# Norm factors applied behind the output projection, memory probabilities turned by VectorE and by way of memory, and a new hand-written order

## The chip, the cores and the metric

The program runs on one core of a Trainium2 chip. A core has a matrix engine (PE, with its weight loads shown as PEld), VectorE (DVE), ScalarE (ACT), GpSimd (POOL) and SyncE (SP, which here only issues DMAs), each with its own in-order instruction queue. The metric is the device time of one execution in microseconds (us); lower is better.

## What is computed

One block of a hybrid model for a sequence of 512 tokens with width 1024: an RMS norm, one wide input projection, four mixers of width 512 next to each other, one output projection, and a last RMS norm.

```python
h = _rmsnorm(x, norm_g[l])
p_fox, p_ssm, p_nsa, p_mem = _split(h @ w_in[l], [FOX_COLS, SSM_COLS, NSA_COLS, MEM_COLS])
mem_kv = _rmsnorm(mem, mem_norm_g[l]) @ w_mem_kv[l]
o = jnp.concatenate([_fox_mixer(...), _ssd_mixer(...), _nsa_mixer(...), _mem_mixer(p_mem, mem_kv)], axis=-1)
x = x + o @ w_out[l]
return _rmsnorm(x, final_norm_g)
```

Two parts matter for the change. The second mixer (mixer 1, the state space mixer) ends in an RMS norm over two groups of 256 columns with a learned gain; the fourth (mixer 3, memory attention, 4 heads of 128) is a plain softmax over 256 memory tokens:

```python
yg = (y * jax.nn.silu(z)).reshape(B, S, SSM_GROUPS, GROUP_W // SSM_GROUPS)
return _rmsnorm(yg, norm_g.reshape(SSM_GROUPS, -1)).reshape(B, S, GROUP_W)
...
s = jnp.einsum('bshd,bmhd->bhsm', q, k).astype(jnp.float32)
pr = jax.nn.softmax(s, axis=-1).astype(v.dtype)
o = jnp.einsum('bhsm,bmhd->bshd', pr, v).reshape(B, S, GROUP_W)
return o * jax.nn.silu(gate)
```

## The kernel before, in words

**Products.** A product in full precision is made of three matmuls (`three`): each operand is split into a rounded high part and the rest (names with h and l: `hh`/`hl`, `wh`/`wl`, `oh`/`ol`). A weight block of 128x1024 is loaded as `raw` (512 KB, by SP), its high part `wh` is made by ACT, and the rest `wl` by a subtraction on POOL or DVE; three `raw`, three `wh` and three `wl` tiles are in turn. `pj` are the PSUM tiles of the input projection, `po` those of the output projection.

**Mixers.** Each mixer is a pipe of stages over its steps (class `Pipe`). The second mixer, `ssm`, has four steps c (128 tokens each). Its stage s3 makes the gated `yc`, s4 the two mean squares `pn` and from them the factors `rsr` (a power on POOL), and s5 spreads these along the free axis by 2 matmuls into PSUM (`prs`, `bcast_rows`) and multiplies four 128x128 pieces by gain and factor (`of<-yc,x,prs` on DVE). `of` is then split into `oh`, `ol`.

**Turning probabilities.** The matmul with the values needs the probabilities with the keys on partitions. In the first and third mixers (probabilities `pF`, `pN`) this is done in two halves: `flip` transposes 32x32 blocks on DVE (STREAM_TRANSPOSE into `fl`), `flip_out` writes each `fl` by 4 DMAs of 64 KB to a scratch tile `farN` in memory, in block order, and `flip_in` reads it back by one DMA of 256 KB as `pt`. In memory attention (`mem`, eight steps, head j and half b2, the probabilities `pM`) the constant MF = 0 lets stage s2 transpose by PE instead: four 128x128 transposes into PSUM (`pT<-cst,pM`), then the split into `pth` (ACT) and `ptl` (DVE). The stages s2o, s2i and s2p, which would go by way of memory for heads j < MF, do nothing.

**Output projection.** `out_proj(mixer, c)` runs over two pairs of token tiles t and over two weight blocks i; a PSUM tile `po` sums all four blocks f of 128 rows, and DVE adds it to the running sum `acc` (`acc<-acc,po`). The last mixer's part (`out_last`) also ends with the final norm.

**Order.** Nothing decides at run time. ORDER says in which order weight blocks are loaded and used; PLAN is a string of steps (a letter for a pipe and the number of its stage; `W` splits a weight block, `L` loads one, `.9` runs nine matmul steps of the foreground); PICKS says for each operation with a choice which engine takes it (V DVE, A ACT, P POOL). All engines' queues follow from the order in which the program text is run through.

Of the kernel before, what the change touches and what calls it, by code (L numbers as in the profile page):

```python
# [44 lines left out]
MF = 0  # L45
# [23 lines left out]
    "f2.5L0.1f3.1f0f2f0f0f2.3W0W0f2.4f3f1.2f1.4f2f2f4.5f3.1f3W0f0f4f0L0.6f4.2f5.1f1L0.3f3.1W0L0.4W0f4f1f0"
    "f2f0f1.6L0L0.5f3f3.6W0W0f0.2f1f1f2.1f2.2f4f4.1W0f3f3s0.1f4f1f4f0f0f0f1f1f1f4f2f2.2f3.5L0L0.4f5f2f2.1"  # L70
    "f2f3f2.4W0W0.6f4L0L0f0L0f3c0.1W0.3f5.1f3f5f5f5f3.5W0.9.1f4f4f5.4f4f4O0f1f5f5L0.1s0s0.3L0f2s1s1.5W0.2"
    "f5W0.2f5f5f3f3s2f5c1f4f5s3f4f5B0f5O0c2O0W0.1O0s1.9.3s0L0W0.3s2s2c3s3L0s3.2L0L0.5s4s1.9.2W0W0.3s2L0s5"
    "W0s3B0B0B0.2L0.3s4L0s4s4.1B0.1W0.9.6W0W0s5s5s5n0n0.7L0.2L0n1.3W0W0.2L0L0L0n0n1n0.1n1.3n2n2n2.8n1W0n3"
    "n0.1n1W0.5n2W0L0n3n4n4n2.4n0n0n3n5n5n3L0.8n1n1W0L0n4n0.2O1O1.2n2.3n3.3n2.2W0.1n3n0.1n0n0n1n1.3O1.3L0"
    ".1L0.3n2W0W0n5.2n1n1n0n0n4n4n4.4L0.1n2W0O1.7n1n1n3n4n2n2n3n3n2n0L0.2n3n3n0n5.5W0n5n3n2.4L0.1n5n3n0n4"
    "n4.1n5n5.4n0n1n4n4n0L0n1n1W0n2n0n2n4.3n1.1n2.3n5L0.4W0.3n5.4n2W0n5n5.3n1n1n3n0n0n0.8L0L0.1n3W0n2n1n1"
    ".4n3n3n3.3n1n4n4n4n4.1W0n5n2W0n5n5n5n0n0n0n0.3n1.1n4.1n2n2.1n2.2L0n3.3W0.9n3.1n1n3.2B0n4n4.2n0L0L0n2"
    ".3L0n4.1n4n1W0n1n2n5n5n3.1W0.2n5.3n0n0n3n1n3.8n2.1n0.3n0W0L0L0n2.5n2n1n5n1n4n4n4n3n1W0n3n3n0n2.2n2n1"
    "n4n4.1n3.3n4W0.9n2.3L0m0m0L0m0.2W0L0.3W0.2n1m1n5m1n5n5n5n4m1n2.2n5n5O2n5n3n3m2.1n2W0.4m2.1m3.1m2.1m3"
    "m3m4n4m0m0m0m0n5m4m4n3n5.1n3.1m5m5O2m1m1n4.1n4m2L0n4n5n5m2L0m1m3m6n5L0m2m5O2O2m3m3m0.2m4.1W0.4m4.5W0"  # L80
    "m4.3m5m5m5m1m1m2W0m6m6m2m3m3.1L0.1L0.3m4m4L0.2m6.4W0.4m6m6.1m5m5.1W0.2m6m6.2W0.9.9.9.9.1"
# [5 lines left out]
    "Rk": "AVVAAVVV",
    "Rl": "VAAAAAVA",
    "ce": "PPVVVV",
    "ct": "AVAAVAVVAAVAVVVA",  # L90
    "kh0": "AVV",
    "kh1": "AVV",
    "ll": "PVPVPPVV",
    "m": "PVVPVPVV",
    "ml": "PVPV",
    "ol": "VVPVPPVPVPPVPPV",
    "pF": "VVVVVVVAVAVVVVAVAAVVVVVAAVVVAVVV",
    "pM": "VAAVVVAAVAVVVAVA",
    "pN": "AVVVAAVVAVAAAAVAVAVAVAAAVVVVVAAVAAVAVVAAAVVVAVAVAAAVAVVAVVAAVVVV",
    "sq": "VPVPVPPV",  # L100
    "wl": "PVPPPPPPPPPPVVVPVPVPPVVVPPPVPPVVPVVPVPPVPVPPVVPVPPVPPPPVVPPPPPVPVPVPPPVV",
    "xde": "VVV",
    "xp": "VVPVVVVV",
    "yc": "PVVVVVVVVVVPVVVP",
# [2047 lines left out]
```

## Time and profile before

| | us |
|---|---|
| median of 3 runs (lowest to highest) | 511.45 (511.14 to 514.05) |
| the profiled execution's own time | 511.3 |
| its span in the trace | 509.5 |
| PE busy | 496.4 |
| DVE busy | 368.9 |
| ACT busy | 297.3 |
| POOL busy | 164.4 |

The span goes from the first to the last instruction of the trace; 1.8 us of the execution's time lie outside it. Busy times are sums over the instructions of an engine, so an engine can be busy for 97% of the span while its instructions overlap. In rows, `out<-in` names the tile written and those read, without their numbers; all lines are L360 since one helper records every operation, and so the tile names tell what an instruction is.

### The profile page before, as it was taken

How to read it: one execution, taken by the hardware profiler on the slowest of the kernel's cores; microseconds unless marked ns; L12 is line 12 of the kernel's file. 1: busy time of each engine (PE TensorE's matmuls, PEld its weight loads, DVE VectorE, ACT ScalarE, POOL GpSimd, SP SyncE). 2: the span in 40 equal slices, each digit the busy share in tenths (PEclk: the TensorE clock that was granted, in tenths of full speed). 3: DMA queues.
4: the chain of work that ended last, by engine and by line, in shares of the span. 5: the costliest groups of instructions: out<-in, count | busy, mean ns of one | idle time of the engine just before them, and what ended most of it. 6: DMA issues, size and time to landing. Idle time of an engine off the chain costs nothing.

```text
span 509.5 us, 8995 instructions
## 1 busy us (share of the span) xinstructions
PE 496.4 (97%) x2965; PEld 419.6 (82%) x2965; DVE 368.9 (72%) x981; ACT 297.3 (58%) x671; POOL 164.4 (32%) x113
## 2 busy tenths in 40 slices
...
GB/s 300 314 326 53 93 85 144 183 79 170 155 262 214 194 228 373 130 171 170 132 152 172 123 225 198 238 219 213 197 196 212 233 233 163 255 138 83 84 41 124
DMA packets 72446, 92.66 MB, mean 182 GB/s; under 512 B 26784, under 2 KB 50624, under 8 KB 72400
## 3 DMA queue, kind: packets, MB, share of 16 engines
...
## 4 chain that ended last, share of the span: by engine, by line
PE 56%; DVE 19%; ACT 9%; DMA 6%; issue 5%; SPq 2%; POOL 2%; POOLq 0%; ACTq 0%; DVEq 0%
PE pj L360 25%; PE po L360 10%; PE pb L360 7%; PE pO L360 5%; PE pS L360 4%; ACT pN L360 3%; DMA raw<-in_wst 3%; DVE wl L360 2%; DVE fl L360 2%; SPq L360 2%; DVE pN L360 1%; DVE xs L360 1%; ACT pF L360 1%; DMA far<-fl 1%; DVE rs L360 1%
## 5 line engine op out<-in xcount | busy, mean ns | idle before, releaser
L360 POOL TENSOR_TENSOR wl<-raw,wh 128x1024 fp32r<-128x1024 f32 (+1 forms) x44 | 109.3, 2493 | 258.9 <-ACT wh L360 182.9
L360 PE MATMUL pj<-hh,wl 128*128 128x512 f32 x352 | 137.6, 391 | 3.5 <-POOL wl L360 2.8
L360 PE MATMUL pj<-hh,wh 128*128 128x512 f32 x352 | 138.5, 393 | 0.5 <-ACT wh L360 0.5
L360 PE MATMUL pj<-hl,wh 128*128 128x512 f32 x352 | 137.2, 390 | 0.0
L360 PEld LDWEIGHTS pj<-hh,wl 128*128 128x128 f32 x352 | 66.1, 188 | 19.1 <-POOL wl L360 3.6
L360 ACT ACTIVATE wh<-raw 128x1024 fp32r<-128x1024 f32 (+1 forms) x72 | 73.3, 1034 | 8.5 <-DMA raw<-in_wst 3.4
L360 PEld LDWEIGHTS pj<-hh,wh 128*128 128x128 f32 x352 | 66.1, 188 | 14.7 <-ACT wh L360 0.9
L360 PEld LDWEIGHTS pj<-hl,wh 128*128 128x128 f32 x352 | 66.1, 188 | 13.0
L360 ACT ACTIVATE pN<-pN,nm 128x128 f32<-128x128 f32 (+7 forms) x96 | 45.3, 473 | 37.5 <-DVE nm L360 36.3
L360 DVE TENSOR_TENSOR wl<-raw,wh 128x1024 fp32r<-128x1024 f32 (+1 forms) x29 | 37.8, 1310 | 4.6 <-ACT wh L360 4.1
L360 PE MATMUL po<-wh,oh 128*128 128x512 f32 x96 | 37.7, 393 | 0.0
L360 PE MATMUL po<-wh,ol 128*128 128x512 f32 x96 | 37.5, 390 | 0.0
L360 PE MATMUL po<-wl,oh 128*128 128x512 f32 x96 | 37.5, 390 | 0.0
L360 ACT ACTIVATE pF<-pF,nm 128x128 f32<-128x128 f32 (+3 forms) x32 | 17.8, 556 | 28.3 <-DVE nm L360 27.4
L360 DVE TENSOR_TENSOR acc<-acc,po 128x512 f32<-128x512 f32 (+1 forms) x33 | 21.1, 663 | 9.9 <-PE po L360 9.8
L360 DVE STREAM_TRANSPOSE fl<-pN 128x128 f32<-128x128 f32 (+3 forms) x64 | 27.9, 482 | 0.1
L360 DVE SCALAR_TENSOR_TENSOR rs<-sm,gat 128x3 f32<-128x3 f32 x32 | 6.6, 206 | 28.8 <-ACT pN L360 28.8
L360 ACT ACTIVATE pN<-pN,rs 128x128 f32<-128x128 f32 (+3 forms) x31 | 16.1, 544 | 12.9 <-DVE rs L360 12.9
L360 DVE CUSTOM_DVE_ANT_0 pN<-pS,bt 128x128 f32<-128x128 f32 (+5 forms) x80 | 22.1, 320 | 0.1
L360 DVE SCALAR_TENSOR_TENSOR xs<-x,cwh,xs 128x512 f32<-128x512 f32 x24 | 19.0, 790 | 4.0 <-ACT xs L360 3.4
L360 PEld LDWEIGHTS po<-wh,ol 128*128 128x128 f32 x96 | 18.0, 188 | 3.8
L360 PEld LDWEIGHTS po<-wl,oh 128*128 128x128 f32 x96 | 18.0, 188 | 3.6
...
## 6 DMA issues: line engine op xcount, KB each, us to landing
raw<-in_wst SPq DMA_DIRECT2D x73, 512.0 KB, 5.0
far<-fl SPq DMA_DIRECT2D x144, 64.0 KB, 2.1
pt<-far SPq DMA_DIRECT2D x36, 256.0 KB, 3.9
...
xn<-in_xn SPq DMA_DIRECT2D x4, 512.0 KB, 7.2
```

The costliest lines, as they stand in the source:

```text
L360: return f(*a, **k)
```

## The change

1. **Second mixer.** Stage s5 goes away. The factors are kept in a fixed tile `rn` (128x8, column 2c + group), written by the same power on POOL. `of` is one 128x512 product of `yc` and gain per step, on DVE or POOL by a new entry in PICKS. `out_proj(1, c)` ends a PSUM sum behind each weight block i (one norm group), and DVE multiplies it by the factor of its token and adds it to `acc` in one instruction: 16 of these in place of 8 additions.
2. **Memory attention.** MF = 4, so all eight steps turn by `flip`, `flip_out` and `flip_in`. 32 PE transposes go; 16 STREAM_TRANSPOSE of 128x256, 32 DMAs of 64 KB, and 8 of 256 KB come; `pth` and `ptl` are made from `pt` in SBUF, `ptl` on four occasions by POOL.
3. **Order.** ORDER, PLAN and PICKS are new throughout. The `strict` flag only skips work of the program that writes the instructions.

```diff
-MF = 0
+MF = 4
...
 PLAN = (
-    "p0.9W0.8L0.5W0.2L0p1W0.7L0L0.2W0.9L0L0.6W0.6W0f0f0f0.6L0L0.3f1.6W0.1W0.5f0L0.4f1.6W0f1.3L0f1L0.6W0.3"
+    ".9W0.5L0.4W0.3L0L0L0.9.2W0W0.5L0.7p0.6W0.2f0f0f0f1.1L0W0p1.4f2.6W0.1f1L0L0L0.2f3.8W0.1f0.1f1f1.2f0.3"
...
 PICKS = {
-    "M": "VAAAVVVA",
+    "M": "AAVAAAAV",
...
+    "of": "VPVP",
...
+    "ptl": "AAVVVAAV",
...
-          "gat": [128, 4, 24], "x0": [128, 632], "cwh": [128, 32], "nacs": [128, 32],
+          "rn": [128, 8], "gat": [128, 4, 24], "x0": [128, 632], "cwh": [128, 32], "nacs": [128, 32],
...
+    rn = C1("rn")
+
     def out_proj(mixer, c):
...
-                        first = f == (0 if t2 == 0 else 2)
-                        hi, lo = o_hl[mixer, t if mixer == 1 else f]
-                        yield max(clock.ready([hi, lo, *w_[i]]), clock.free_banks(1) if first else 0.0)
+                        first = f % 2 == 0 if mixer == 1 else f == (0 if t2 == 0 else 2)
+                        yield 0.0 if state.get("strict") else max(
+                            clock.ready([*o_hl[mixer, t if mixer == 1 else f], *w_[i]]), clock.free_banks(1) if first else 0.0)
...
-                        out_mm(p[x], mixer, t, f, w_[i], cs, (0, 3) if t2 == 0 else (2, 1))
+                        out_mm(p[x], mixer, t, f, w_[i], cs,
+                               (2 * i, 2 * i + 1) if mixer == 1 else (0, 3) if t2 == 0 else (2, 1))
...
-            for x in range(2):
+                for x in range(2) if mixer == 1 else ():
+                    t = 2 * t2 + x
+                    a = acc[t][:, 512 * c:512 * c + 512]
+                    V.scalar_tensor_tensor(out=a, in0=p[x], scalar=rn[:, 2 * t + i:2 * t + i + 1], in1=a,
+                                           op0=OP.mult, op1=OP.add)
+            for x in range(2) if mixer != 1 else ():
                 a = acc[2 * t2 + x][:, 512 * c:512 * c + 512]
                 V.tensor_tensor(out=a, in0=a, in1=p[x], op=OP.add)
...
-            st[c] = (yc, rsq(pn[:, 0:2], 2, 1.0 / 256, "rs"))
-
-        def s5(c):
-            yc, r = st.pop(c)
-            pr = PS("prs")
-            bcast_rows(pr, r, 2)
+            rsq(pn[:, 0:2], 2, 1.0 / 256, "rs", rn[:, 2 * c:2 * c + 2])
             of = o_f[1, c] = G("of")
-            for j in range(4):
-                jc, gc = slice(j * 128, (j + 1) * 128), slice(j // 2 * 128, (j // 2 + 1) * 128)
-                V.scalar_tensor_tensor(out=of[:, jc], in0=yc[:, jc], scalar=v_sg[:, j:j + 1], in1=pr[:, gc],
-                                       op0=OP.mult, op1=OP.mult)
+            tt(0, out=of.rearrange("p (j l) -> p j l", j=4), in0=yc.rearrange("p (j l) -> p j l", j=4),
+               in1=v_sg[:, :, None].to_broadcast([128, 4, 128]), op=OP.mult)
```

**Order on PE, near the end.** In the kernel before, the last PV products of NSA (`pO<-pt,nv`, the third mixer; `ct` are its compressed keys' probabilities) stand between the transposes of memory attention (`pT<-cst,pM`):

```order
L360 MATMUL pO<-pth,mvl 128x256
L360 MATMUL pT<-cst,pM 128x128 x8
L360 MATMUL pO<-ct,vcm 64x128 x2
L360 MATMUL pO<-pt,nv 64x128 x12
L360 MATMUL pO<-ct,vcm 64x128 x2
L360 MATMUL pO<-pt,nv 64x128 x16
L360 MATMUL pT<-cst,pM 128x128 x4
L360 MATMUL pO<-pth,mvh 128x256
```

After the change no transpose stands there; the first weight blocks of the third mixer's output projection (`po<-wh,oh`) follow directly on the last NSA product:

```order
L363 MATMUL pj<-hl,wh 128x512
L363 MATMUL pj<-hh,wl 128x512
L363 MATMUL pO<-ct,vcm 64x128 x2
L363 MATMUL pO<-pt,nv 64x128 x16
L363 MATMUL po<-wh,oh 128x512
L363 MATMUL po<-wl,oh 128x512
```

What moved: the transposes are gone from PE, and the output projection of the third mixer has come up to the last NSA product.

**Order on SP, near the end.** Before, the last turned tiles (scratch tiles far_5317 and far_5322, the last two of NSA) are written and read, and all weight loads that are left follow in one go:

```order
L360 DMA far_5317<-fl 32x4x128 x4
L360 DMA far_5322<-fl 32x4x128 x4
L360 DMA pt<-far_5282 128x512
L360 DMA pt<-far_5287 128x512
L360 DMA pt<-far_5317 128x512
L360 DMA pt<-far_5322 128x512
L360 DMA raw<-in_wst 128x1024 x6
```

After the change the last four tiles of NSA are far_5299, far_5304, far_5317 and far_5322; far_5241, far_5395 and far_5479 are tiles of memory attention, and a weight load (`raw`) stands behind them:

```order
L363 DMA far_5299<-fl 32x4x128 x4
L363 DMA far_5304<-fl 32x4x128 x4
L363 DMA pt<-far_5241 128x512
L363 DMA far_5317<-fl 32x4x128 x4
L363 DMA far_5322<-fl 32x4x128 x4
L363 DMA pt<-far_5299 128x512
L363 DMA pt<-far_5304 128x512
L363 DMA far_5395<-fl 32x4x128 x4
L363 DMA pt<-far_5317 128x512
L363 DMA pt<-far_5322 128x512
L363 DMA far_5479<-fl 32x4x128 x4
L363 DMA raw<-in_wst 128x1024
```

What moved: nothing stood between the last turned tiles of NSA and the weight loads before; now tiles of memory attention are mixed in with them.

**Order on DVE, near the end.** After the change, the eight last flips of memory attention and two gate products (`sg`) stand at the end of six softmax steps (`nm`, `rs`, `pM`), and ahead of a weight split `wl` for the third mixer's output projection:

```order
L363 TENSOR_REDUCE nm<-pS 128x2
L363 RECIPROCAL rs<-sm 128x2
L363 TENSOR_SCALAR pM<-pM,rs 128x256
L363 STREAM_TRANSPOSE fl<-pM 128x2x4x32 x8
L363 SCALAR_TENSOR_TENSOR sg<-sg,pj 128x512
L363 SCALAR_TENSOR_TENSOR sg<-pO,sg 128x512
L363 TENSOR_TENSOR wl<-raw,wh 128x1024
L363 TENSOR_TENSOR ptl<-pt,pth 128x512 x2
```

Before, the row `wl` stands ahead of the softmax steps there, directly behind two flips of NSA:

```order
L360 STREAM_TRANSPOSE fl<-pN 128x4x4x32 x2
L360 TENSOR_TENSOR wl<-raw,wh 128x1024
L360 SCALAR_TENSOR_TENSOR ql<-pj,qh 128x512
L360 TENSOR_REDUCE nm<-pS 128x2
L360 RECIPROCAL rs<-sm 128x2
L360 TENSOR_SCALAR pM<-pM,rs 128x256
```

What moved: six softmax steps and their flips now stand ahead of the split, where the split stood ahead of them.

## Rows read from the trace of the kernel before

**Rows 1.** The profile's page of the kernel before: the totals by engine (busy us, share of the span, instructions), and the shares of the chain of work that ended last.

```profile
PE 496.4 (97%) x2965; PEld 419.6 (82%) x2965; DVE 368.9 (72%) x981; ACT 297.3 (58%) x671; POOL 164.4 (32%) x113
...
PE 56%; DVE 19%; ACT 9%; DMA 6%; issue 5%; SPq 2%; POOL 2%; POOLq 0%; ACTq 0%; DVEq 0%
```

**Rows 2.** Busy time of each engine in stretches of the run: the stretch in us, its length, then busy us (and instructions) of PE, PEld, DVE, ACT and POOL, PE's granted clock, DMA share and GB/s.

```profile
110.00:130.00 20.00, 17.48 (x80) 13.77 (x79) 15.73 (x40) 15.94 (x31) 2.61 (x2) 1.00 0.46 126
130.00:240.00 110.00, 110.00 (x748) 93.20 (x747) 87.72 (x189) 57.01 (x125) 34.78 (x24) 1.00 0.66 209
240.00:250.00 10.00, 8.72 (x39) 6.88 (x38) 8.85 (x14) 7.67 (x15) 4.78 (x4) 1.00 0.33 130
...
310.00:320.00 10.00, 9.24 (x46) 7.54 (x44) 7.12 (x33) 5.80 (x25) 1.42 (x3) 1.00 0.76 226
...
430.00:470.00 40.00, 40.00 (x296) 35.27 (x295) 23.11 (x43) 23.86 (x58) 10.53 (x6) 1.00 0.54 175
```

**Rows 3.** The waits of PE by what ended them: us in total, how often, the longest (the first five).

```profile
PE pj L360 <- POOL wl L360: 2.8, 2, 1.5
PE pw L360 <- DVE warm L360: 1.3, 1, 1.3
PE pO L360 <- ACT ct L360: 0.8, 1, 0.8
PE pj L360 <- DVE wl L360: 0.5, 1, 0.5
PE pj L360 <- ACT wh L360: 0.5, 1, 0.5
```

**Rows 4.** Timeline of PE in two places (start, length, instruction and how many in a row; starts, not lengths, show what one costs, since each overlaps the next): the memory transposes at 433 us, and the memory's PV product behind 453 us.

```profile
433.07 1.04 PE L360 MATMUL pT<-cst,pM 128*128 128x128 f32 x8
434.03 0.44 PE L360 MATMUL pO<-ct,vcm 96*64 96x128 f32 x4
...
434.96 1.04 PE L360 MATMUL pO<-pt,nv 128*64 128x128 f32 x16
435.94 0.66 PE L360 MATMUL pT<-cst,pM 128*128 128x128 f32 x4
436.35 0.47 PE L360 MATMUL pj<-hh,wh 128*128 128x512 f32 x1
436.66 0.39 PE L360 MATMUL pj<-hl,wh 128*128 128x512 f32 x1
436.89 0.40 PE L360 MATMUL pj<-hh,wl 128*128 128x512 f32 x1
...
453.63 0.28 PE L360 MATMUL pO<-pth,mvl 128*128 128x256 f32 x1
453.75 0.28 PE L360 MATMUL pO<-pth,mvh 128*128 128x256 f32 x1
```

**Rows 5.** Groups of instructions by engine, operation, tiles and shape, of the whole run: x how many | busy us, mean ns of one | idle time of the engine just before them and what ended it. First those that the change takes away or turns, then those whose durations price what it adds.

```profile
L360 PE MATMUL pT<-cst,pM 128*128 128x128 f32 x32 | 4.4, 276 | 0.0
...
L360 PE MATMUL prs<-cst,rsr 128*128 128x128 f32 x16 | 2.1, 275 | 0.0
...
L360 DVE SCALAR_TENSOR_TENSOR of<-yc,x,prs 128x128 f32<-128x128 f32 x16 | 4.3, 342 | 0.0
...
L360 DVE TENSOR_TENSOR acc<-acc,po 128x512 f32<-128x512 f32 x31 | 20.3, 679 | 9.9 <-PE po L360 9.8
...
L360 DVE TENSOR_TENSOR ptl<-pT,pth 128x512 fp32r<-128x512 f32 x8 | 5.1, 684 | 3.6 <-ACT pth L360 3.6
...
L360 DVE STREAM_TRANSPOSE fl<-pN 128x512 f32<-128x512 f32 x16 | 10.2, 683 | 0.0
...
L360 DVE STREAM_TRANSPOSE fl<-pN 128x256 f32<-128x256 f32 x16 | 6.1, 417 | 0.0
...
L360 ACT ACTIVATE wh<-raw 128x1024 fp32r<-128x1024 f32 x69 | 71.6, 1052 | 8.5 <-DMA raw<-in_wst 3.4 <-issue 1.7 <-POOL rx L360 1.4
...
L360 DVE TENSOR_TENSOR wl<-raw,wh 128x1024 fp32r<-128x1024 f32 x27 | 36.4, 1357 | 4.6 <-ACT wh L360 4.1
...
L360 POOL TENSOR_TENSOR wl<-raw,wh 128x1024 fp32r<-128x1024 f32 x42 | 106.2, 2538 | 250.7 <-ACT wh L360 174.6 <-PE pO L360 24.1 <-DVE ql L360 16.8
```

**Rows 6.** Timeline of SP's own queue of DMA issues near its end (start, length, how many in a row), and then, of the DMA issues by kind, KB each and the median us from issue to landing.

```profile
437.69 3.81 SPq L360 DMA_DIRECT2D far<-fl  x8
441.60 1.82 SPq L360 DMA_DIRECT2D pt<-far  x4
...
raw<-in_wst SPq DMA_DIRECT2D x73, 512.0 KB, 5.0
far<-fl SPq DMA_DIRECT2D x144, 64.0 KB, 2.1
pt<-far SPq DMA_DIRECT2D x36, 256.0 KB, 3.9
```

**Rows 7.** Timeline of DVE in the softmax of memory attention (start, length, instruction; in brackets the idle time ahead of it and what ended it).

```profile
427.61 0.69 DVE L360 TENSOR_REDUCE nm<-pS 128x2 f32<-128x512 f32 x1 [1.23 <-PE pS L360]
429.39 0.17 DVE L360 RECIPROCAL rs<-sm 128x2 f32<-128x2 f32 x1 [1.09 <-ACT pM L360]
429.59 0.35 DVE L360 TENSOR_SCALAR pM<-pM,rs 128x256 f32<-128x256 f32 x1
429.86 0.68 DVE L360 TENSOR_REDUCE nm<-pS 128x2 f32<-128x512 f32 x1
```

More of the change, by code (lines that the diff above doesn't have):

```diff
@@ L67 @@
 PLAN = (
-    "p0.9W0.8L0.5W0.2L0p1W0.7L0L0.2W0.9L0L0.6W0.6W0f0f0f0.6L0L0.3f1.6W0.1W0.5f0L0.4f1.6W0f1.3L0f1L0.6W0.3"
[L69 to L81, printed above, removed]
+    ".9W0.5L0.4W0.3L0L0L0.9.2W0W0.5L0.7p0.6W0.2f0f0f0f1.1L0W0p1.4f2.6W0.1f1L0L0L0.2f3.8W0.1f0.1f1f1.2f0.3"
@@ new lines @@
+    "s0.4W0f2.8W0.5f4.1f1L0.3f2f3W0f3f2.1s0f0L0f0.1f4.2f4.7W0f1.4f1.5L0.1L0.1f3.2f2.1W0W0f0.3L0.1f3.1f5L0"
+    ".2f2.2f0f0.5f1.1f5.2W0L0f2f3f1f1f3.1f0f2L0f0f1.1W0.2f1.3f2.3f4W0f4f4.4f2f2.8f0f4f3f0f1f0L0f1f1.5W0.3"
+    "f0f3f3f5W0f1.1L0f3f2f2.2f4.4f3f4f4L0.1f5.4f5f5W0f5f5.4f3f2.1L0f4f4W0L0f2f4f3f3.1f4.1f4O0.4f5.1f5O0f2"
+    ".1W0.4s0L0f5.5f5f5f5.1W0.3f3.2c0s1s1.2W0.1L0.6f4.1c1s1.1W0.1s0f5O0s2f5s2.3L0.6O0L0L0s3s3s2.4W0.3c2s3"
+    "s1.1s2L0.6W0.5W0.1B0.5W0.2c3L0L0L0s3B0B0B0.3B0.1B0.6W0.4W0.6W0.2s4s4n0.3L0W0.3L0L0.1W0n1.4n0.1n0.4L0"
@@ new lines @@
+    "L0.3n1s4.5O1n2n1W0W0n2n3.1n2n0n0s4.3n1.1W0.4L0.2n1n3n3n0n0n2n2n4.5n4n5n1.7n3L0W0L0.1n3W0n2n1.1n0.1n5"
+    ".2L0.1n0n0n0n0L0n1.2n4.6O1O1.2n5.1n2.1n4n4.4O1n1n1n3n1n1n2W0W0.4n3n2L0n2.1W0n0n0.3n4n5n5.5L0n2.3n5n1"
+    "n4W0n3L0.1n2.3n3L0.3n2n0n3n3n1n0.5n2n1n3.2W0n0n4n0n2.6n5.1n3n1L0.1W0n2.1n1.2W0n0.2n4.1n4.2n5.1n3n4n3"
+    ".1n4n0n1n1n0.3n5n2L0L0W0n4.3n5.1n1n4n2n3n2.2n1.1L0.3n5.2n3n2n3n5n3n2W0n0n0.9.1n1n3n4n4n5n4W0n1.1n4n4"
+    "W0L0n0n0.4n2.9.2n5n3n3W0n1n0.2L0L0n0n1.4n4.3n2n2n1L0n1n5.2n2W0.1W0n0n0.2n5.4n3.1n1n1n5.1n2.2L0.1W0.2"
@@ L82 @@
+    "n0n0.4n2n3.2n5n5.6L0.1W0n2L0.1n3n3W0n4n2.1n1m0n0n4n4n5n4m1n5m0.2n4n5.1m1.1n5.8n3n2n3W0n3m2n1n1m0n3n4"
+    ".1m2.1O2.1m0m1m3m4m0n2m1.1m3n2n5.3n3.1O2n4.4m0m0m2m0m1m1m1n4n4O2n4n4m1m5m4n3n5n5m2n5n5n5.3L0n5n4n5n5"
+    "m3.1m3.1W0.2m4m4m5.1m2m2O2m3m3L0L0m5L0m5.7m6.2m4.1m2m4m5W0W0m5m3.1m6m6m6m6.5m4L0m2L0m6.4W0m3.1m4.9m5"
+    "m5m6L0W0W0.6m6.9.9.9W0.5"
 )
 PICKS = {
-    "M": "VAAAVVVA",
[L87 to L104, printed above, removed]
+    "M": "AAVAAAAV",
+    "Rk": "VAVVAVAA",
+    "Rl": "VAAVAVVA",
@@ new lines @@
+    "ce": "PVPPVV",
+    "ct": "VAAAAAAAAVVAAAVA",
+    "kh0": "VVV",
+    "kh1": "VAV",
+    "ll": "VVPPVVVV",
+    "m": "VVVPPVVP",
+    "ml": "PVPP",
+    "of": "VPVP",
+    "ol": "VVPPPPPPPPPVVPV",
+    "pF": "AAVAAAAAVAAAVVVVAAVAAVVVAAAAVAVV",
+    "pM": "AAVAVAAAAAVVAAVA",
+    "pN": "VAAVVAAAAAVAAAVAVAAVAVVAAAAVAVAAAAVVAAAAVVVVAVVAVVAVAVAAAVAVVVVA",
+    "ptl": "AAVVVAAV",
+    "sq": "PPVPVPPP",
+    "wl": "PVPPPPPPPPVPVPPVVPVPVPPVVVPVVPPPVVVVVVVPVVPVVPPPPPPVVPPPPPPPPPPVPPPPPVVV",
+    "xde": "PVV",
@@ L105 @@
+    "xp": "PVVVVPPP",
+    "yc": "VPPPVVVVPPVVPVPV",
 }
@@ L1127, in out_last @@
             for f in range(4):
+                v = [x[f % 2] for x in w_[f // 2]]
+                yield 0.0 if state.get("strict") else max(clock.ready([*o_hl[LAST, t if LAST == 1 else f], *v]),
+                                                          clock.free_banks(1) if f == 0 else 0.0)
                 hi, lo = o_hl[LAST, t if LAST == 1 else f]
-                v = [x[f % 2] for x in w_[f // 2]]
-                yield max(clock.ready([hi, lo, *v]), clock.free_banks(1) if f == 0 else 0.0)
                 if f == 0:
```

6 lines of the change are left out of this document (2 added, 4 removed), and 16 rows, old and new, of the table ORDER.

## The prediction

> **What bounds the kernel now.** I read the page's totals first: PE is busy for 97% of the span and the chain that ended last is for 56% PE's own work, DVE's 19% coming next [rows 1]. A busy share is only a sum of lengths, so the stretches come second. From 130 to 240 us PE is busy 110.00 of 110 us and from 430 to 470 us 40.00 of 40, at full granted clock, while DVE has 22 and 17 us spare in the same stretches; gaps show in few places only, 2.5 us in 110 to 130, 1.3 in 240 to 250, 0.8 in 310 to 320 [rows 2]. Third, the waits of PE say what they are: 2.8 us on two splits `wl` by POOL, 0.8 on `ct`, 0.5 and 0.5 on `wl` and `wh`, and 1.3 on the start-up's `warm`, which nothing here touches [rows 3]. So PE's queue bounds the run nearly everywhere: a matmul taken away is worth what lies between its start and the next one's, and work for other engines costs nothing until something that PE needs becomes late.
>
> One rule speaks against this reading. The Trainium skill (Perfetto Trace Analysis, Identifying the Most-Contended Engine) holds that the busy share of matmuls is a poor measure, as they are pipelined, and that of weight loads a good one. By it PE is filled to 82% [rows 1], and the removed matmuls might lie in the other 18%. The trace disagrees where it counts: starts follow each other without a gap [rows 4], and the listed waits are 1% of the span [rows 3].
>
> **Taken from PE.** 32 transposes `pT<-cst,pM` and 16 records `prs` (8 matmuls, two records each), all 128 columns wide, go [rows 5]. Their lengths, 4.4 and 2.1 us busy [rows 5], count overlap; starts are better. Eight transposes take 434.03 - 433.07 = 0.96 us up to the next instruction, four take 436.35 - 435.94 = 0.41 [rows 4], so 0.10 to 0.12 us each. I take 0.11: 32 x 0.11 = 3.5 us and 16 x 0.11 = 1.8 us, together 5.3 us (bounds 4.8 by the four transposes and 6.5 by the lengths).
>
> The Trainium skill (VectorE: DVE Perf Modes, The three transpose paths) gives a 128x128 transpose 390 ns on TensorE and 311 on VectorE, in 32x32 blocks only, and its rules for authors would leave it with TensorE. By that figure 32 transposes would be 12.5 us, and my sum 9 us lower than with 3.5. The starts decide: a transpose costs a busy PE 0.11 us, not 0.39 [rows 4], and the rule's preference is the slower rival below.
>
> **Given to PE.** The new order has 17 runs of 64-wide matmuls (`pO<-pt`, `pY` and the like) where there were 14. Going into such a run costs up to 0.14 us (the eight transposes took 0.96 instead of twice 0.41), coming out 0.08 (the first `pj` takes 436.66 - 436.35 = 0.31, the second 0.23) [rows 4]. At 0.2 us a run: +0.6 us (0 to 1).
>
> **Moved to DVE, ACT and POOL.** The second mixer loses 16 products of 0.34 us on DVE (5.5 us), and gets two of 128x512, each near 0.68 by the addition of that shape, and 8 more combinations into `acc` at 0.68 [rows 5]: 1.4 + 5.4 - 5.5 = +1.3 us. The other two products fall to POOL. Memory attention adds 16 flips at 0.417 and loses four `ptl` at 0.684 [rows 5]: +4.0 us. All this lies beside PE work, mostly in stretches where DVE is busy for about 80% or less [rows 2]. Without that cover the second mixer's combinations would cost 5.4 us, since PE waits for a PSUM bank behind each; two token tiles' matmuls (12 of 0.23 us) stand between two of them, so I take nothing.
>
> **The waits that the change adds.** Each of eight memory steps now costs SP 4 + 1 issues. Twelve issues took 3.81 + 1.82 = 5.63 us, 0.47 each [rows 6], so 40 more are 18.8 us of SP. They all fall to the end, where the order rows show five memory tiles around the last four of NSA and ahead of a weight load. I follow two chains to that weight's `wl`, from the last four NSA flips on.
>
> PE's work from the memory scores ahead of them to the use of `wl`, counted in the new order: 52 matmuls of 512 columns at 0.23, 48 of 256 columns at 0.12, and 96 records of 64-wide ones at 0.06 [rows 4]: 12.0 + 5.8 + 5.8 = 23.5 us. DVE may begin the flips 0.7 us ahead of this, so 24.2 us are there.
>
> DVE: four flips of 512 (2.7 us), six softmax steps at 429.86 - 427.61 = 2.25 each, of which 1.09 is waiting for ACT [rows 7] (13.5), twelve memory flips at 0.417 (5.0), four `sg` of the size of an `acc` addition, 0.68 (2.7), then `wl` 1.36 [rows 5]: 25.3 us. PE waits 1.1 us. Nothing else can go first, for the queue is in order.
>
> SP: 29 issues stand between the first of these four tiles and the end of the line before the weight load, 29 x 0.47 = 13.6 us; landing 5.0 [rows 6]; `wh` 1.05, `wl` 1.36 [rows 5]: 21.0 us behind the first flip. That fits by some 2.5 us if SP is free when the flip is done. Ahead of it stand 22 issues for older tiles in the new order, 10.3 us; if half of them are still open, PE waits 2 to 3 us, with all of them 7 to 8. The last `pt` of NSA has the same queue: first far to fourth `pt` are 4 + 4 + 1 + 8 + 2 + 4 + 2 = 25 issues, 11.8 us, plus 3.9 to land [rows 6]. What is late next is the six `po` groups behind the `wl`.
>
> So the tail costs between 1 and 8 us. I take 2.5: DVE's 1.1 is nearly certain, and SP's backlog is worked off while DVE goes through the softmax steps.
>
> **The rest of the order.** 4.6 us of waits outside start-up [rows 3] are shuffled. None of them is bound to the removed work; the bounds are -4.6 and +4.6. The long ones hang on a POOL split of 2.5 us right ahead of its use [rows 3, 5]. In the new order I find no POOL split with as little room, and several on DVE that are short by some tenths; I take -1.2 us.
>
> **Sum.** 511.3 (the profiled execution's own time, 509.5 span and 1.8 outside; the median is 511.45, so no correction) - 5.3 + 0.6 + 2.5 - 1.2 = 507.9, told as 508.0.
>
> **Rivals.**
> - *More comes back.* The tail hides (DVE's softmax steps come out shorter as ACT's 1.09 us wait is filled by flips between them) and the shuffled waits mostly go: 511.3 - 5.3 + 0.6 - 3 = 503.6 us. For it: two waits alone are 2.8 us [rows 3]. Against it: an order this dense makes new ones.
> - *No change worth the name.* The removed PE work returns as waiting at the tail: SP with most of its backlog open costs 5 to 6 us, so 511 to 512. For it: SP's twelve issues were back to back [rows 6]. That the removed matmuls were not on the path gives the same time, and speaks little for itself [rows 2].
> - *Slower.* One mechanism: SP as the turning point of memory attention. Every `pt` has to wait until its four `far` have landed, 2.1 us [rows 6], and nothing else on SP may pass. Where no other tile's issues stand between, a tile holds SP for 5 x 0.47 + 2.1 = 4.5 us, eight for 36 us, on a queue that was back to back there already [rows 6] and that has the weight loads to issue too. It decides from 10 us of lateness beyond the sum's 2.5: about 518 us. Against it: tiles are interleaved in the order, so most landings are covered.
>
> **How the numbers follow.** Forecast (506.3 to 510.5): 0.48. More comes back (503 to 506.3): 0.28. No change worth the name (510.5 to 515): 0.16. Slower (over 516.6): 0.08. A difference under 1%, 5.1 us, can hardly be told from no change, so faster by over 1% (below 506.3) is 0.28, the middle 0.48 + 0.16 = 0.64, slower 0.08. For 8 in 10 the range leaves out the lower part of the second case and the last with the upper end of the third: 503.8 to 512.6. The forecast's own range is 506.3 to 510.5.
>
> **What would show it.** In the changed profile PE's busy time falls by about 5 us, and no `pT<-cst,pM` or `prs` is left. PE's waits list a `wl` near 440 us of 1 to 5 us, ended by DVE, or a `pt` of NSA; the waits in 110 to 130 and 240 to 250 us are gone. `acc` on DVE has 16 entries with `rn` and no wait of PE for a bank behind them. SP's queue is solid from 400 to 450 us. Wrong would be: waits for `po` banks in the second mixer's projection, a PE wait on `ptl` of several us, or new waits above 5 us in the first 300 us, which I have not priced one by one.

## The result, and the profile after

The changed kernel takes 507.0 us in the median (506.24 to 507.64, 4 runs) beside 511.75 us (511.14 to 514.05, 4 runs) for the kernel before on the same chip: a ratio of 0.9899, 95% interval 0.9871 to 0.9928. On two further chips the same program stood at 510.35 us, ratio 0.9912 (0.9882 to 0.9943), and 510.66 us, ratio 0.9945 (0.9923 to 0.9967). The gain is there each time, between 0.5 and 1.0%, where 0.7% was forecast (511.3 to 507.9 us).

All rows up to the experiments are from the profiled execution of the first chip: 506.91 us, span 505.1 against 509.5 before. First the page's totals by engine and its chain of work, which answer to [rows 1].

```profile
PE 491.9 (97%) x2917; PEld 414.3 (82%) x2917; DVE 361.5 (72%) x952; ACT 308.4 (61%) x695; POOL 174.3 (35%) x130
...
PE 73%; DVE 11%; ACT 8%; DMA 4%; issue 3%; POOL 0%; POOLq 0%; ACTq 0%; SPq 0%; DVEq 0%
```

PE has lost 48 records, the 32 transposes and the 16 of `prs`, and 4.5 us of busy time. Its own work is now 73% of the chain where it was 56%: the kernel is bound by PE still, and more so.

The same stretches as in [rows 2], and one new one, 280 to 290 us (columns as there):

```profile
110.00:130.00 20.00, 20.00 (x93) 16.73 (x92) 12.42 (x26) 15.54 (x30) 4.82 (x2) 1.00 0.65 202
130.00:240.00 110.00, 109.08 (x731) 91.59 (x730) 91.56 (x187) 63.22 (x134) 31.95 (x29) 1.00 0.62 194
240.00:250.00 10.00, 10.00 (x52) 7.96 (x53) 8.64 (x12) 6.20 (x13) 3.78 (x3) 1.00 0.21 70
280.00:290.00 10.00, 8.00 (x41) 6.56 (x40) 8.33 (x26) 8.00 (x19) 7.17 (x5) 1.00 0.50 144
310.00:320.00 10.00, 10.00 (x68) 8.18 (x67) 6.88 (x37) 7.82 (x27) 0.67 (x1) 1.00 0.81 241
430.00:470.00 40.00, 40.00 (x282) 34.85 (x281) 25.74 (x52) 22.22 (x53) 11.20 (x9) 1.00 0.72 213
```

The three gaps of before are closed, and the end of the run, where the prediction put its new wait, is as full as it was. Instead 0.9 us are missing from 130 to 240 and 2.0 us from 280 to 290, and 1.7 us from 60 to 70, where PE was busy for 10.00 us before. PE's waits (total, how often, longest), answering to [rows 3], name what is new:

```profile
PE pT L363 <- DVE nm L363: 2.0, 1, 2.0
PE pj L363 <- DVE wl L363: 1.4, 2, 0.9
PE pw L363 <- DVE warm L363: 1.3, 1, 1.3
PE pj L363 <- ACT wh L363: 1.2, 1, 1.2
```

The POOL splits (2.8) and `ct` (0.8) are gone; a wait in the scaling of NSA's compressed probabilities (2.0), `wl` on DVE (1.4 where 0.5 was) and `wh` (1.2 where 0.5 was) have come. The 1.2 us stand at 65.7 us, behind a weight block that landed at 64.6. On the two further chips the same block landed at 66.0, and this wait is 2.5 and 2.6 us there; behind it the granted clock from 70 to 80 us is 0.86 and 0.88, where it is 1.00 on the first chip. By an estimate (1.3 to 1.4 us more of waiting, and 0.12 to 0.14 of 10 us by the clock) that is up to 2.8 of the 3.4 to 3.7 us between the chips; the kernel before is 3.7 and 1.8 us longer there too, and why was not looked into.

**Where 4.4 us came from.** I took for each PE record the distance from its start to the next one's start, and the median of that distance over all records with its tiles and shape. The medians sum to 486.1 us before and 480.2 after (-5.9). What exceeds them by over 0.18 us, the waits, is 7.2 before and 7.1 after (-0.2). What exceeds them by 0.015 to 0.18 us is 26.1 and 27.3 (+1.3). Most of this lies within runs of 64-wide matmuls; the going into and out of such runs is 4.8 and 6.2 of it, and so the whole rise. What stays below the medians makes the last +0.4. The last matmul starts at 502.99 and 498.59 us: -4.4, the sum of the four.

**The new wait of 2 us.** Timeline of three engines at 286 us (start, length, engine, instruction; in brackets the idle time ahead of it):

```profile
283.56 4.71 POOL L363 TENSOR_TENSOR wl<-raw,wh 128x1024 fp32r<-128x1024 f32 x2
...
286.22 2.20 DVE L363 TENSOR_SCALAR pcp<-pN,rs 128x16 f32<-128x16 f32 x1
...
290.73 0.24 DVE L363 TENSOR_SCALAR pcp<-pN,rs 128x24 f32<-128x24 f32 x1
...
288.56 0.29 PE L363 MATMUL pT<-cst,pcp 128*96 128x128 f32 x1 [2.00 <-DVE nm L363]
```

A DVE product of 16 columns takes 2.20 us, where the next of its kind, of 24 columns, takes 0.24. It starts within the second of two weight splits on POOL and ends, at 288.42, just behind it (283.56 + 4.71 = 288.27). PE waits for nothing else here; the profile names `nm`, the DVE instruction that ended at that moment, but what the matmul reads is `pcp`. The Trainium skill (SBUF — State Buffer, SBUF: two separate sides) says that DVE's instructions in a two-port mode or with two SBUF inputs and GpSimd's instructions share one pair of ports as an exclusive lock, which whoever starts first keeps "for the whole instruction". These rows fit it; the experiments test it.

**The tail.** DVE, SP, ACT and PE from the last four NSA flips to the weight split on which the prediction laid its 2.5 us, answering to [rows 4, 6, 7]:

```profile
429.35 2.48 DVE L363 STREAM_TRANSPOSE fl<-pN 128x512 f32<-128x512 f32 x4
...
447.60 2.73 DVE L363 STREAM_TRANSPOSE fl<-pM 128x256 f32<-128x256 f32 x8
450.24 0.65 DVE L363 SCALAR_TENSOR_TENSOR sg<-sg,pj 128x512 f32<-128x512 f32 x1
450.81 0.68 DVE L363 SCALAR_TENSOR_TENSOR sg<-pO,sg 128x512 f32<-128x512 f32 x1
451.41 1.21 DVE L363 TENSOR_TENSOR wl<-raw,wh 128x1024 fp32r<-128x1024 f32 x1
...
446.51 0.38 SPq L363 DMA_DIRECT2D raw<-in_wst  x1
...
449.93 1.06 ACT L363 ACTIVATE wh<-raw 128x1024 fp32r<-128x1024 f32 x1 [0.58 <-DMA raw<-in_wst]
...
453.63 0.39 PE L363 MATMUL po<-wl,oh 128*128 128x512 f32 x1
```

From the first flip to the end of `wl` DVE takes 452.62 - 429.35 = 23.3 us; PE uses it at 453.63, 24.3 us behind that flip. So 1.0 us is left where the prediction had 1.1 too few. The `raw` behind the far tiles came early enough for PE: `wh` was made at 450.99, and PE uses it at 453.40.

Last, three groups of DVE that answer to [rows 5] (busy us, mean ns of one | idle time before):

```profile
L363 DVE SCALAR_TENSOR_TENSOR acc<-po,rn,acc 128x512 f32<-128x512 f32 x16 | 11.0, 734 | 0.0
L363 DVE STREAM_TRANSPOSE fl<-pM 128x256 f32<-128x256 f32 x16 | 5.8, 415 | 0.1
L363 DVE TENSOR_SCALAR pcp<-pN,rs 128x16 f32<-128x16 f32 x8 | 3.8, 480 | 0.6
```

The second mixer's additions with the factor cost 734 ns each, near the 0.68 assumed, and no wait of PE for `po` stands behind them. Flips of 128x256 have the mean of [rows 5], but their lengths overlap: eight in a row take 2.73 us, 0.34 each.

### The profile page after: what moved, and what is told of

Its sections match the earlier page's. It is cut to its first block, busy times and chain, and to the rows that moved or that the text cites. A ratio compares the mean times of both kernels' runs of the same rounds, so it can differ in the third digit from the quotient of the medians.

```text
span 505.1 us, 8962 instructions
## 1 busy us (share of the span) xinstructions
PE 491.9 (97%) x2917; PEld 414.3 (82%) x2917; DVE 361.5 (72%) x952; ACT 308.4 (61%) x695; POOL 174.3 (35%) x130
## 4 chain that ended last, share of the span: by engine, by line
PE 73%; DVE 11%; ACT 8%; DMA 4%; issue 3%; POOL 0%; POOLq 0%; ACTq 0%; SPq 0%; DVEq 0%
PE pj L363 33%; PE po L363 17%; PE pO L363 7%; PE pb L363 6%; PE pS L363 4%; DMA raw<-in_wst 2%; ACT pF L363 2%; DVE wl L363 2%; ACT wh L363 2%; PE pW L363 1%; PE pY L363 1%; DVE fl L363 1%; ACT M L363 1%; ACT pN L363 1%; ACT L L363 1%
## 5 line engine op out<-in xcount | busy, mean ns | idle before, releaser
L363 POOL TENSOR_TENSOR wl<-raw,wh 128x1024 fp32r<-128x1024 f32 (+1 forms) x43 | 102.4, 2387 | 208.3 <-ACT wh L363 133.3
L363 ACT ACTIVATE pN<-pN,rs 128x256 f32<-128x256 f32 (+3 forms) x36 | 19.4, 563 | 14.8 <-DVE rs L363 14.8
L363 DVE SCALAR_TENSOR_TENSOR xs<-x,cwh,xs 128x512 f32<-128x512 f32 x24 | 22.2, 926 | 5.7 <-ACT xs L363 5.0
L363 DVE TENSOR_TENSOR acc<-acc,po 128x512 f32<-128x512 f32 (+1 forms) x25 | 16.1, 660 | 9.2 <-PE po L363 9.0
L363 ACT ACTIVATE th<-xs 128x512 f32<-128x512 f32 x8 | 5.1, 633 | 26.4 <-DVE xs L363 26.4
```

Source lines behind the costliest of these rows:

```text
L363: return f(*a, **k)
```

## The experiments

Twelve runs on three further chips: nine different edits, one of them run twice, and the changed kernel itself twice. Each ratio is to the kernel before on the same chip. Runs 1, 2, 3 and 5 were made on one chip (before: 513.54 us), 8, 9 and the first pair of 6 on another (515.48 us), 4, 7 and the second pair of 6 on a third (513.59 us). On the first of these the changed kernel itself was not run, so runs 1 and 5 are compared with it by their ratios alone (0.990 to 0.9945 on the other chips).

**1. The PE work put back by other means.** The memory scores are issued twice, which adds 48 matmuls of 256 columns and nothing for other engines.

```diff
             for i in range(2):
...
-                three(p[:, i * 256:(i + 1) * 256], (qh[:, qs], ql[:, qs]), (kh, kl), True, True, 0)
+                for _ in range(2):
+                    three(p[:, i * 256:(i + 1) * 256], (qh[:, qs], ql[:, qs]), (kh, kl), True, True, 0)
```

> The changed kernel with the score matmuls of memory attention issued twice (the second time over the first, with the same values): 48 matmuls of 256 columns more on PE, 48 x 0.12 = 5.8 us, about as much as the change took away, and nothing else. Theory (the gain is PE work taken off a queue that is the bound): the time rises by 5.5 to 6 us over the changed kernel's 507.0, to about 512.8, ratio to the kernel before 1.002. Rival (the new order brought the gain, and PE had room): it rises by less than 2 us.

515.22 us, ratio 1.0022 (1.0001 to 1.0043). The gain is gone, with work that no other engine sees. Against the changed kernel's ratios elsewhere the added matmuls cost 0.8 to 1.2%, 4.0 to 6.3 us, where their distances make 5.8. So PE's queue is the bound of the changed kernel where they stand, and a matmul there is worth its distance to the next start.

**2. The second mixer's part alone, in the old order.** The kernel before with `rn`, the one product `of` per step and the additions with the factor; ORDER and PLAN as before (the code of part 1 of the change, with one line added to PICKS; stage s5 stays, without `prs`).

```diff
+    "of": "VPVP",
...
-            st[c] = (yc, rsq(pn[:, 0:2], 2, 1.0 / 256, "rs"))
+            st[c] = (yc, rsq(pn[:, 0:2], 2, 1.0 / 256, "rs", rn[:, 2 * c:2 * c + 2]))
```

> The kernel before, in its old order, with the second mixer's part of the change alone: factors in rn, no prs matmuls, 16 combinations into acc. Theory: PE loses 8 matmuls of two records at 0.11 us each, 1.8 us, and DVE's 8 more combinations cost nothing: ratio 0.9965, about 509.9 us. Rival (DVE's combinations hold PSUM banks and PE waits for them): at 8 x 0.68 us at most 5.4 us come back, ratio 1.000 to 1.007.

521.69 us, ratio 1.0145 (1.0121 to 1.0169): it does not gain 1.8 us but loses some 8, more than either forecast. PE has its 16 records less (2949), but its waits, counted as above, are 18.6 us where they were 7.2. Some of them, from the view of waits (the first was there before, [rows 3]):

```profile
PE pj L361 <- POOL wl L361: 2.8, 2, 1.5
PE pW L361 <- DVE sg L361: 2.2, 1, 2.2
PE pj L361 <- DVE wl L361: 1.9, 4, 0.6
...
PE pT L361 <- DVE pcp L361: 1.2, 2, 1.0
```

Waits for a bank of the second mixer's projection, which the rival expected, are 0.4 us of it (`po` for `acc`). The 2.2 us for `sg` come from a hold of the same kind as at 286 us: at 367 us DVE's `wl` takes 3.44 us, and a POOL split that starts with it 2.38.

```profile
366.99 3.44 DVE L361 TENSOR_TENSOR wl<-raw,wh 128x1024 fp32r<-128x1024 f32 x1
...
366.96 2.38 POOL L361 TENSOR_TENSOR wl<-raw,wh 128x1024 fp32r<-128x1024 f32 x1 [14.59 <-DVE L L361]
```

**3. Memory attention by way of memory alone, in the old order.**

```diff
-MF = 0
+MF = 4
```

> The kernel before, in its old order, with MF = 4 alone: memory attention turned by DVE and by way of memory. Theory: 3.5 us of PE work go; the old order leaves 11 to 17 us from the place of a transpose to its use, and the way by memory needs about 11 (flips 0.8, issues 1.9, landing 2.1, read 0.5 and 3.9, the two casts 1.3), more where SP's queue is long: 0 to 6 us of waits come back, so 508 to 514 us; I take 510, ratio 0.997. Rival (only the new order makes room for it): over 514 us, ratio above 1.006.

531.85 us, ratio 1.0347 (1.0298 to 1.0397): the rival. The execution in the trace is the slowest of the four, 536.06 us. PE's timeline in two places, the two rows of SP that matter for the first, and then the stretches (columns as in [rows 2]):

```profile
455.51 0.58 PE L360 MATMUL pO<-pth,mvh 128*128 128x256 f32 x1 [4.30 <-ACT pth L360]
...
457.04 0.41 PE L360 MATMUL pO<-ptl,mvh 128*128 128x256 f32 x1
457.25 0.41 PE L360 MATMUL pO<-pth,mvl 128*128 128x256 f32 x1
465.92 0.58 PE L360 MATMUL pO<-pth,mvh 128*128 128x256 f32 x1 [8.25 <-ACT pth L360]
...
443.20 8.64 SPq L360 DMA_DIRECT2D far<-fl  x16
...
451.89 0.45 SPq L360 DMA_DIRECT2D pt<-far  x1
```

```profile
450.00:460.00 10.00, 3.23 (x12) 2.08 (x10) 2.14 (x5) 3.45 (x11) 0.00 (x0) 0.77 0.70 196
460.00:470.00 10.00, 3.94 (x26) 3.42 (x28) 6.80 (x18) 5.61 (x15) 2.50 (x2) 0.50 0.15 50
470.00:480.00 10.00, 10.00 (x81) 9.03 (x79) 3.11 (x6) 3.41 (x8) 0.00 (x0) 0.88 0.89 271
```

The old order has the values' matmuls as soon behind the scores as the old transposes allowed. By way of memory the tiles come later: SP issues the `pt` for the first wait behind sixteen writes in a row, and ACT's `pth` for the second stands in its queue behind four softmax steps, up to 465.26 us. PE waits 4.3 and 8.2 us. These waits cost twice: from 460 to 470 us the granted clock is 0.50, its lower level of 1.2 GHz, and 256-wide matmuls start 0.21 us apart instead of 0.12. What memory attention needs comes too late, as in the prediction's slower rival, but not by its mechanism: SP is issuing from 443.20 to 451.84 us and does not stand waiting for a landing.

**4. The old way in the new order.** The changed kernel with PE's transposes back in memory attention.

```diff
-MF = 4
+MF = 0
```

> The new order and the new second mixer stay, memory attention turns its probabilities by PE again (MF = 0): what the way by memory is worth inside the new order. Theory (PE is the bound, each transpose costs 0.11 us, and what the memory attention tail waits for comes with the transposes): 32 transposes are 3.5 us, and where twelve of them stand directly behind the softmax steps PE waits for the last pM, some 4 us more; together 0.7 to 1.5% above the changed kernel. Rival (the transposes lie in gaps of PE, and what made the gain is the new order with the second mixer's part alone): no difference, within 0.2%. SP's queue is free in the tail, so no wait on raw there.

525.46 us, ratio 1.0218 (1.0184 to 1.0252); the changed kernel stood at 510.66 on this chip, so 2.9% more, twice the upper end of what I expected. The profiled run (521.53 us, the fastest) shows 11.7 us of the 14.8: 32 records more, the granted clock down to 0.83 in 450 to 460 us, and two new waits.

```profile
PE pT L363 <- DVE pM L363: 3.9, 3, 2.9
PE pT L363 <- ACT pM L363: 2.8, 2, 1.8
```

The transposes now stand where nothing separates them from the softmax. The executions without a profile are 3 to 6 us longer again; their mean granted clock is 0.984 to 0.987 beside 0.993 in the profiled one, which by an estimate (0.6 to 0.9% of 525 us) is 3 to 5 us. Where it was lost was not settled. Together with run 3: neither way of turning can do with the other's order.

**5. The wait at 286 us: is it the memset?** `pcp`'s tile is cleared by POOL ahead of it; here DVE clears it.

```diff
-                P.memset(st["c"], 0.0)
+                V.memset(st["c"], 0.0)
```

> The changed kernel with the zeroing of pcp done by DVE in place of POOL. In the changed kernel DVE's write to pcp at 286 us lasted 2.20 us in place of 0.23 and ended just behind POOL's zeroing, which stood behind two splits of 4.71 us; PE waited 2.0 us. Theory: that wait goes, 16 zeroings of about 0.1 us on DVE cost nothing: 505.0 us, ratio 0.986. Rival (the long write has another cause, such as the two engines' shared access to memory): no change, 507.0.

512.01 us, ratio 0.9966 (0.9944 to 0.9987), and the product is as long as before: 2.07 us, again within two POOL splits (287.52 to 292.22).

```profile
290.18 2.07 DVE L363 TENSOR_SCALAR pcp<-pN,rs 128x16 f32<-128x16 f32 x1
...
287.52 4.70 POOL L363 TENSOR_TENSOR wl<-raw,wh 128x1024 fp32r<-128x1024 f32 x2
```

My theory that the memset held it fell. What is left is the split. (The time alone shows little here, since the changed kernel was not run on this chip.)

**6. The changed kernel again, and the one product on ACT.** For comparison the changed kernel as it is ran on both of the other chips, with the fourth `pcp` scaling (the one at 286 us) on ACT beside it.

> The changed kernel once more, as it is, so that the next three and the kernel before are compared with it on one chip. Both theories: a ratio of 0.988 to 0.993, as first measured.

> The changed kernel as it is, for comparison on this chip. On two chips it stood at 0.990 and 0.991 of before; 0.989 to 0.993 is expected here. By the reading of the first run its profile shows a 2 us wait of PE for nm near 288 us again, and in the tail between 0 and 1.5 us of waits on wl or wh.

```diff
-            V.tensor_scalar(out=pcp[:, 64 * a:64 * a + nc_], in0=tc_, scalar1=rs[:, 0:1], scalar2=None, op0=OP.mult)
+            st["n"] = st.get("n", -1) + 1
+            if st["n"] == 3:
+                A.activation(pcp[:, 64 * a:64 * a + nc_], tc_, AF.Copy, scale=rs[:, 0:1])
+            else:
+                V.tensor_scalar(out=pcp[:, 64 * a:64 * a + nc_], in0=tc_, scalar1=rs[:, 0:1], scalar2=None, op0=OP.mult)
```

> The changed kernel with one instruction of DVE, the scaling into pcp at 286 us, done by ACT. Its length of 2.20 us in place of 0.23 ended with POOL's split, and zeroing pcp on DVE did not shorten it. Theory (DVE's scaling and POOL's split take turns at SBUF, and the later one waits for the whole of the other): PE's wait of 2.0 us goes, 505.0 us, 0.4% under the changed kernel on the same chip. Rival (a wait for something else that ends at that moment): no change.

> The version with the one pcp scaling on ScalarE once more, beside the changed kernel. If the hold of VectorE behind POOL's split at 286 us costs the run its whole 2 us, this is 0.4% below the changed kernel on the same chip; the last comparison had 0.25%. Rival: PE catches the 2 us up later, since VectorE is ahead by then, and the two are equal within 0.1%.

The changed kernel's ratio of 0.9945 on the second chip lies outside the 0.989 to 0.993 that I expected there. With the product on ACT: on the first of the two chips 509.07 us, ratio 0.9881 (0.9851 to 0.9912), beside 510.35 for the changed kernel: 0.25% less. On the second 508.16 us, ratio 0.9902 (0.9868 to 0.9937), beside 510.66: 0.49% less, more than the 0.4% of a whole 2 us. The intervals of the pairs overlap, but both pairs and the profiles say the same: ACT's product takes 0.31 us at 289.22 and PE's wait falls from 2.2 to nothing listed on the one chip, from 1.9 to 0.4 on the other. This version has the lowest median on both chips.

The changed kernel's profile on the first of these chips shows the tail wait after all. PE's timeline there, then ACT's `wh`:

```profile
457.21 0.50 PE L363 MATMUL po<-wh,oh 128*128 128x512 f32 x1 [0.43 <-ACT wh L363]
458.47 0.50 PE L363 MATMUL po<-wl,oh 128*128 128x512 f32 x1 [0.76 <-DVE wl L363]
...
456.10 1.06 ACT L363 ACTIVATE wh<-raw 128x1024 fp32r<-128x1024 f32 x1 [3.54 <-DMA raw<-in_wst]
```

SP issued that `raw` at 451.14 us. So 1.2 us of the predicted wait are there on this chip, by way of SP and the weight's landing, and none on the other two.

**7. One POOL split on DVE.** The other side of the same test: POOL's second split moves, `pcp` stays.

```diff
-    "wl": "PVPPPPPPPPVPVPPVVPVPVPPVVVPVVPPPVVVVVVVPVVPVVPPPPPPVVPPPPPPPPPPVPPPPPVVV",
+    "wl": "PVPPPPPPPPVPVPPVVPVPVPPVVVPVVPPPVVVVVVVPVVPVVPPVPPPVVPPPPPPPPPPVPPPPPVVV",
```

> The changed kernel with one weight split (the second of POOL's two from 283.6 us on) on VectorE, everything else in place. Theory (VectorE and POOL take turns at SBUF, the one that starts first keeps it for its whole instruction): the split on VectorE starts within POOL's first split and takes not 1.23 us but about 2 to 3.2, as it is held until POOL ends at about 285.9; pcp then takes 0.2 to 0.3 us again instead of 2.2, as POOL is idle behind it. It ends 0.3 to 1.5 us later than before the edit, so PE's wait near 288 us is between 1.5 and 3.5 us and the time is that of the changed kernel within 0.3%. Rival (pcp is slow for another reason, such as its own tile or what the memset does): pcp still takes about 2.2 us and the split takes 1.23.

```profile
288.35 2.87 DVE L363 TENSOR_TENSOR wl<-raw,wh 128x1024 fp32r<-128x1024 f32 x1 [0.24 <-ACT wh L363]
...
293.40 0.23 DVE L363 TENSOR_SCALAR pcp<-pN,rs 128x16 f32<-128x16 f32 x1
...
287.75 2.39 POOL L363 TENSOR_TENSOR wl<-raw,wh 128x1024 fp32r<-128x1024 f32 x1
```

As the theory had it: the split on DVE starts within POOL's and ends 1.08 us behind its end, after 2.87 us, and `pcp`, with POOL idle, takes 0.23. The rival is out. The time, 513.76 us and ratio 0.9999 (0.9977 to 1.0021), is 0.6% above the changed kernel where I expected 0.3% at most: PE waits 3.3 us for `nm` instead of 1.9, and 0.9 for `acc` behind another hold, at 372 us (two `pN` products in 2.96 us beside a POOL split of 2.40). That names 2.3 of the 3.1 us; other listed waits are 0.7 us shorter than in the changed kernel's trace, so half of the loss is not accounted for.

**8. How much room the tail has on DVE.** The last four memory tiles are flipped twice.

```diff
-                V.transpose(out=to[:, s], in_=tiles[c + s].rearrange("p (b j x) -> p b j x", b=b, j=4))
+                for _ in range(2 if twice else 1):
+                    V.transpose(out=to[:, s], in_=tiles[c + s].rearrange("p (b j x) -> p b j x", b=b, j=4))
...
-                st[s] = flip([t[:, i * 256:(i + 1) * 256] for i in range(2)], 256, 1)
+                st[s] = flip([t[:, i * 256:(i + 1) * 256] for i in range(2)], 256, 1, s[0] >= 2)
```

> The changed kernel with the flips of memory attention's last four tiles done twice (the same values again): 8 STREAM_TRANSPOSE of 0.35 us more on DVE ahead of the split wl at 451.4 us, 2.8 us. Theory (DVE's chain ends 1.0 us ahead of PE's use, 452.6 against 453.6): PE waits 1.8 us more. Rival (the tail has several us of room): no change.

513.7 us, ratio 0.9969 (0.9943 to 0.9996), 3.4 us above the changed kernel. The execution in the trace is the fastest of the ten, 512.42 us. The eight flips are sixteen and take 6.56 us, and PE waits at the predicted place, 0.9 us longer than I expected, since the second eight cost 3.8 us and not 2.8:

```profile
450.10 6.56 DVE L363 STREAM_TRANSPOSE fl<-pM 128x256 f32<-128x256 f32 x16
...
457.76 1.21 DVE L363 TENSOR_TENSOR wl<-raw,wh 128x1024 fp32r<-128x1024 f32 x1
...
459.01 0.50 PE L363 MATMUL po<-wl,oh 128*128 128x512 f32 x1 [2.72 <-DVE wl L363]
```

3.8 us more on DVE give 2.7 us of waiting: 1.1 us of room, as the first profile had it (1.0). Beside the changed kernel's trace on this chip, which has 1.2 us of waits there (run 6), the rise is 1.5 us.

**9. How much room it has on SP.** Two tiles ahead of the weight load are written twice, eight issues more.

```diff
-            for i in range(4):
+            for i in 2 * [0, 1, 2, 3] if state["far"] in (75, 76) else range(4):
```

> The changed kernel with the eight DMAs that write two memory tiles ahead of the weight load at 446.5 us issued twice: 8 x 0.47 = 3.8 us more on SP's queue. The weight landed at 449.9 us, wh and wl need 1.06 + 1.21 us, PE uses wl at 453.6: 1.4 us of room. Theory (SP's queue is solid there): PE waits 2.4 us more. Rival (SP has pauses that take it up): no change.

517.51 us, ratio 1.004 (1.0011 to 1.007), 7.2 us above the changed kernel: three times what I expected. The execution in the trace is the slowest of the ten, 520.58 us. In it PE waits 2.5 us for `wh` at 463.20, 0.7 for `wl`, and 1.6 for the last `pt` of NSA, 4.8 together where the changed kernel's trace on this chip has 1.2. Behind them the clock is lower:

```profile
450.00:460.00 10.00, 8.41 (x72) 6.72 (x69) 5.18 (x14) 3.91 (x11) 2.51 (x2) 1.00 0.50 135
460.00:470.00 10.00, 6.78 (x26) 5.62 (x25) 3.47 (x5) 4.11 (x7) 1.05 (x1) 0.68 0.84 276
```

From 460 to 470 PE is granted 0.68 in the mean, a part of the stretch at the lower level. By an estimate (0.32 of 10 us) that costs up to 3.2 us, which with 3.6 us more of waits comes near the 7.2. So 3.8 us more on SP cost twice what 3.8 us more on DVE cost (run 8), because a wait there is paid a second time by the clock.

## Why the prediction was right, and where not

The sum came to 507.9 us and 507.0 was measured, by terms that were off on both sides. The mechanism, PE work taken off a full queue, is borne out; that the number fits so well is partly luck, since the tail's +2.5 us did not come and about as much was missed by the terms for 64-wide runs and for waits (0.7 and 1.0 us) and by small ones.

- **PE bounds the run (right).** Run 1 gives the gain back with PE work alone. By the Trainium skill's measure (Perfetto Trace Analysis, Identifying the Most-Contended Engine), the busy share of weight loads, 82%, the removed matmuls might have lain in spare time. The trace disagrees: the last start came 4.4 us earlier.
- **-5.3 us of PE work (right).** The 48 records are gone; the medians' sum fell by 5.9, of which 48 x 0.11 = 5.3 are theirs. (The 390 ns that the prediction quotes for a transpose is the page's figure for bf16; those here are f32.)
- **+0.6 for more 64-wide runs (too small by half).** +1.3 measured, for three more runs, as counted.
- **+2.5 in the tail (mis-sized: 0 on the first chip).** The place and both chains were right, as runs 8 and 9 show, and on one other chip 1.2 us of it appeared. DVE needed 23.3 us where the sum had 25.3. Flips were taken at 0.417, a mean of lengths that overlap, where they take 0.34 in a row (12 x 0.08 = 0.9 us); `wl` at 1.36, a mean that held ones lengthen (below), where it takes 1.21; the rest is in the softmax steps, taken at 2.25 with a wait for ACT that other work partly filled, as the rival of more coming back had it. PE's side of the comparison was right: 24.3 us from the first flip to the use of `wl`, where 24.2 were counted.
- **-1.2 of shuffled waits (wrong).** They came to -0.2: 4.6 us of waits went and about as many came. On the two further chips the new ones in the first 300 us are 6.1 and 5.9 us (`wh` at 67 us, `nm`, `wl`), above the 5 us that the prediction named as a sign of being wrong. The largest on the first chip, 2.0 us, has a cause that the prediction did not consider: DVE held behind a POOL split. Runs 5, 6 and 7 show it, by leaving the memset out as a cause, by moving DVE's product away (the wait ends) and by moving the split (it is then the one to be held). The prediction looked for POOL splits late for PE; this one was in time, and in another engine's way. The trace of the kernel before had such holds already: five of the 27 `wl` on DVE in [rows 5] took 1.70 to 2.20 us each, which is why their mean is 1357 ns, and an `ol` took 1.46 us instead of 0.68 and ended 0.55 us behind the second of three splits (440.19):

```profile
435.41 7.59 POOL L360 TENSOR_TENSOR wl<-raw,wh 128x1024 fp32r<-128x1024 f32 x3 [16.84 <-DVE ql L360]
...
439.29 1.46 DVE L360 TENSOR_TENSOR ol<-sg,oh 128x512 fp32r<-128x512 f32 x1
```

- **The second mixer's additions (right in the new order only).** No PE wait stands behind the 16. In the old order the same code costs 8 us (run 2), 10 us from the 1.8 that its matmuls are worth. How many of them are the code's and how many those of an order not made for it was not separated.
- **DVE's load (not counted in full).** By the prediction's moves DVE's busy time would rise by 5.3 us; it fell by 7.4, while ACT's rose by 11.1 and POOL's by 9.9. The new PICKS, which the sum left out, moved more work than the two parts did.
- **Slower (right to refuse).** In the new order SP does not hold memory attention up on the first chip. Run 3 shows a lateness of that size, 18 us, in the old order, though by long queues on SP and ACT and not by tiles that stand one by one for their landing. That interleaving is what prevents it in the new order was not tested.

What each part is worth alone is not a meaningful number: part 1 costs 1.5% and part 2 3.5% in the old order, and without part 2 the new order is 2.2% above the kernel before. Of the combinations tried only the three together gain. The new order with the second mixer's part undone was not tried, nor the new order alone.
